# Queries and keys of two attentions, made transposed by the projection itself

## The chip, the core and the metric

One core of one Trainium2 chip runs the whole program. The metric is device time in microseconds (us) for one execution. A row of the profile names engines as PE (TensorE, matrix products), PEld (its loading of weights), DVE (VectorE), ACT (ScalarE), POOL (GpSimd) and SP (the engine that issues most DMAs).

## The reference, cut to what matters

The program is a first transformer block (gated linear attention and block attention side by side, cross attention to a memory, 32 experts) and then two hybrid layers (differential attention and stick-breaking attention side by side, a gated feed-forward), for 256 tokens of width 1024 in float32. The change touches the queries and keys of block attention (once) and of stick-breaking attention (once per layer):

```python
h = x * rsqrt(mean(x * x) + eps) * g          # per token
q_m, k_m, v_m = h @ w_in[:, 1552:2064], h @ w_in[:, 2064:2576], h @ w_in[:, 2576:3088]
o_m = moba_attention(q_m, k_m, v_m, rel_bias) # 8 heads of 64, q scaled by 64 ** -0.5
...
sq, sk, sv = h @ w_in_2[l][:, 1536:2048], h @ w_in_2[l][:, 2048:2560], h @ w_in_2[l][:, 2560:3072]
o_sb = stick_breaking_attention(sq, sk, sv)   # 8 heads of 64, scores q . k / 8
```

Both attentions need q and k with the head's 64 columns on the partitions (transposed: 4 strips of 128 columns by 256 tokens), since scores sum over them.

## The kernel before

Tokens lie in two tiles of 128 (NT = 2, T = 256). A norm (class `Norm`) keeps the transposed activations x * g, without the factor per token, in a high and a low half that together make float32 (`xs`, 8 slices of 128 by 256 tokens). The factor per token, `nrm.scale(t)`, is a column of 128 numbers, applied when a product is read out of PSUM.

A projection to 512 columns is `dense` (L324). Weights come in four chunks of 256 rows (KC = 2 slices); ScalarE makes their high half (L295, `wh`), VectorE the low half (L300, `wl`), and each pair of slices and tokens takes three matmuls (high by high, low by high, high by low, L334). Activations are stationary (128x128), 512 columns of weights move. One projection is 4 chunks x 2 token tiles x 3 x 2 slices = 48 matmuls, accumulated in two PSUM tiles of the pool `psm` (four buffers), one per token tile. In the last chunk token tile 0 is finished first and read out by `evac(0)`, then tile 1.

For queries and keys `evac` is `rows_T` (L572): the product is scaled by the token's factor into `rows` (VectorE, L267, for tile 0; ScalarE, L265, for tile 1), and TURN = 20 products later `to_T` (L566) transposes it in four 128x128 steps on TensorE (L569) and copies the result into qTm, kTm, sqT or skT (ScalarE, L570).

Work beside the projections is put among their products by hand: `soon(n, fn)` runs `fn` when n more products have been issued (`passed()` counts them), and `keep` fixes the order on an engine. TensorE runs in exactly this order. In the first block the order around the change is: projection of query (products 1 to 48), key (49 to 96), value (97 to 144), counted from the start of the query's. `gla_out(t)` (L535, output of linear attention, with a norm over its result: ScalarE L547, VectorE L549, GpSimd L178, VectorE L551) is put at 80 and 104, and `moba_scores(j)` (L598, for the head pairs j = 0 to 3) at 96 + 28 + 20 j. Both take PSUM tiles named "at" from the pool `psa`, which has two buffers: `gla_out` one, `moba_scores` two. In the layers the scores of differential attention (`diff_scores`, L1387) and later those of stick-breaking attention (L1449) are put in the same manner, and take "at" tiles too.

Two places serve as a comparison below. `decay_down` (L403) already has weights stationary and 256 tokens moving. `decay_up` has one "at" tile of two halves, and between the two products into it VectorE reads the first half:

```python
pl = new(psa, [P, NT, 256], name="at")
for t in range(NT):
    keep(mm(pl[:, t], alT[:, t * P:(t + 1) * P], wal, start=True, stop=True))           # L411
    nc.vector.scalar_tensor_tensor(la[:, t], pl[:, t], n1.scale(t), bal, ...)           # L412
```

Of the kernel before, what the change touches and what calls it, by code (L numbers as in the profile page):

```python
# [17 lines left out]
ALU = mybir.AluOpType  # L18
AX = mybir.AxisListType

P = 128
T = 256
NT = T // P
D = 1024
KD = D // P
KC = 2
# [2 lines left out]
AT_GATES = 4  # L29
AT_MERGE = (1, 1, 1, 1, 1, 1)  # L30
LAG = 3
EARLY = 24
OVER = 5
TAIL = (6, 12, 13, 15)
# [8 lines left out]
MOBA = 20  # L43
TURN = 20
# [66 lines left out]
def forward(ctx: ExitStack, tc: tile.TileContext, a: dict, out: bass.AP):  # L111
    nc = tc.nc
    mm = nc.tensor.matmul
# [9 lines left out]
    psm = ctx.enter_context(tc.tile_pool(name="psm", bufs=4, space=bass.MemoryType.PSUM))  # L123
    pst = ctx.enter_context(tc.tile_pool(name="pst", bufs=2, space=bass.MemoryType.PSUM))
    psa = ctx.enter_context(tc.tile_pool(name="psa", bufs=2, space=bass.MemoryType.PSUM))
    dram = ctx.enter_context(tc.tile_pool(name="dram", bufs=1, space=bass.MemoryType.DRAM))

    def new(pool, shape, dt=F32, name="t", **kw):
        return pool.tile(shape, dt, name=name, tag=name, **kw)
# [38 lines left out]
    cst = ctab.get  # L168
    ident = cst("ident")
# [93 lines left out]
    def scaled(dst, src, r, eng):  # L263
        if eng == "s":
            nc.scalar.activation(dst, src, AF.Copy, scale=r)  # L265
        else:
            nc.vector.tensor_scalar(dst, src, r, None, op0=ALU.mult)  # L267

    def keep(ins):
        return tc.keep_in_program_order(ins)  # L270
# [5 lines left out]
    def load(parts, kc, n, pool=wraw, tag="raw"):  # L276

        raw = chunk(pool, tag, kc, n)
        at = 0
        for src in parts:  # L280
            w = src.shape[1]
            nc.sync.dma_start(out=raw[:, :kc, at:at + w], in_=src.rearrange("(k p) n -> p k n", p=P))
            at += w
        return raw
# [18 lines left out]
    def halves(raw, kc, n, *order):  # L303

        h = high(raw, kc, n, *order)
        return h, low(raw, h, kc, n, *order)

    def wload(parts, kc, n):
        return halves(load(parts, kc, n), kc, n)
# [3 lines left out]
    def soon(n, fn, *args):  # L313

        waiting.append((products[0] + n, fn, args))

    def passed():
        products[0] += 1
        due = [v for v in waiting if v[0] <= products[0]]
        waiting[:] = [v for v in waiting if v[0] > products[0]]  # L320
        for _, fn, args in due:
            fn(*args)

    def dense(xs, parts, n, evac, tail=1, loaded=None, order=free):  # L324

        nk = len(xs)
        ps = [new(psm, [P, 512], name="mm") for _ in range(NT)]
        step = KC if n == 512 else nk
        chunks = [(k0, min(step, nk - k0)) for k0 in range(0, nk, step)]

        def go(t, k0, kc, wh, wl):
            for i, (part, ww) in enumerate(((0, wh), (1, wh), (0, wl))):
                for k in range(kc):
                    order(mm(ps[t][:, :n], xs[k0 + k][part][:, t * P:(t + 1) * P], ww[:, k, :n],  # L334
                             start=(k0 == 0 and i == 0 and k == 0), stop=(k0 + kc == nk and i == 2 and k == kc - 1)))
                    passed()

        held = []
        for c, (k0, kc) in enumerate(chunks):
            ww = wload([p[k0 * P:(k0 + kc) * P, :] for p in parts], kc, n)  # L340
            if c < len(chunks) - tail:
                for t in range(NT):
                    go(t, k0, kc, *ww)
            else:
                held.append((k0, kc, *ww))
        if loaded:
            loaded()
        for t in range(NT):
            for c in held:
                go(t, *c)  # L350
            evac(t, ps[t])

    def add_to_x(xs, W, then=None, loaded=None, order=free):
        for half in range(2):
            hs = slice(half * 512, (half + 1) * 512)

            def evac(t, ps):
                nc.vector.tensor_add(x[:, t, hs], x[:, t, hs], ps)
                if then:
                    then(x[:, t, hs], t, half)  # L360

            dense(xs, [W[:, hs]], 512, evac, 3 if half else 1, loaded and functools.partial(loaded, half), order)
# [5 lines left out]
    n1 = Norm(gmix)  # L368
# [8 lines left out]
    w_in = a["w_in"][0]  # L377
# [5 lines left out]
    me = mix1.enter_context(tc.tile_pool(name="mixe", bufs=1))  # L383
# [53 lines left out]
    def rows_into(dst, nrm):  # L437
        return lambda t, ps: scaled(dst[:, t], ps, nrm.scale(t), "sv"[t])
# [13 lines left out]
    def evac(t, pp):  # L452
        qk = new(tmp, [P, 512], name="rows")
        scaled(qk, pp, n1.scale(t), "s")
        soon(TURN, gla_turn, t, qk)
# [110 lines left out]
    def to_T(src, dst, t, scale, order):  # L566
        ps = new(pst, [P, 4, P], name="tp")
        for k in range(4):
            order(nc.tensor.transpose(ps[:, k, :], src[:, k * P:(k + 1) * P], ident))  # L569
        nc.scalar.activation(dst[:, :, t * P:(t + 1) * P], ps, AF.Copy, scale=scale)  # L570

    def rows_T(dst, nrm, scale=1.0, lag=0):  # L572
        def evac(t, pp):
            qm = new(tmp, [P, 512], name="rows")
            scaled(qm, pp, nrm.scale(t), "vs"[t])
            if lag:
                soon(lag, to_T, qm, dst, t, scale, keep)
            else:
                to_T(qm, dst, t, scale, free)
        return evac  # L580
# [11 lines left out]
    sums = new(me, [P, NT, 8], name="sums")  # L592
# [47 lines left out]
    soon(20 + 14 * 4, nmem.done)  # L640
    for t in range(NT):
        soon(TURN * 2 + 40 + 24 * t, gla_out, t)
    for i, dst in ((0, qTm), (1, kTm)):
        dense(n1.xs, [w_in[:, 1552 + 512 * i:2064 + 512 * i]], 512, rows_T(dst, n1, 0.125 if i == 0 else 1.0, TURN), order=keep)
    for j in range(4):
        soon(TURN + 8 + MOBA * j, moba_scores, j)
    dense(n1.xs, [w_in[:, 2576:3088]], 512, rows_into(vm, n1), order=keep)

    dense(nmem.xs, [w_ckv[:, 0:512]], 512, rows_T(kTc, nmem, lag=TURN), order=keep)
    dense(nmem.xs, [w_ckv[:, 512:1024]], 512, rows_into(vc, nmem), order=keep)  # L650

# [90 lines left out]
    def prefetch(n):  # L742
        ahead.extend(load_rows(src, *nextraw()) for src in itertools.islice(upcoming, n))
# [30 lines left out]
    with tc.tile_pool(name="crossp", bufs=1, reuse_waits="tile", side="right") as cp:  # L774
        qTc = new(cp, [P, 4, T], name="qTc")
        dense(n2.xs, [a["w_cq"][0]], 512, rows_T(qTc, n2, 128.0 ** -0.5), tail=2)

        pm = []
        for h in range(4):
            ps = new(psm, [P, NT, T], name="mm")  # L780
# [50 lines left out]
        def feed_moe(src, t, half):  # L831
# [14 lines left out]
            if half and t:  # L846
                logits(0, 1)

        add_to_x(slices(oT), a["w_co"][0], feed_moe, lambda half: half and prefetch(GROUP))
        ss = new(sml, [P, NT], name="s2")  # L850
        nc.vector.tensor_add(ss, ssm[:, 0], ssm[:, 1])
# [17 lines left out]
    def s3(name, n):  # L869
        return new(mp, [P, NT, n], name=name)  # L870
# [5 lines left out]
    before, ones = counting[:, 0], counting[:, 1]  # L876
# [12 lines left out]
    order, down_from = cst("order"), cst("down_from")  # L889
# [33 lines left out]
    for g in range(2):  # L923
        xsT.append(new(mp, [P, KD, GROUP * 32], name="xs%d" % g))
        if g == 0:
            wt = s3("wt", 32)
            prefetch(EARLY - GROUP)
    hT = {}
# [209 lines left out]
    sums = []  # L1138
# [188 lines left out]
    def heads8(v):  # L1327
        return v.rearrange("p (h d) -> p h d", h=8)

    def layer(l, nrm, nxt):  # L1330
        lam_init = 0.8 - 0.6 * math.exp(-0.3 * l)
        W = a["w_in_2"][l]
        tc.keep_in_program_order(nc.scalar.preload_act_table_set("natural_log_exp_and_others"))
        with tc.tile_pool(name="attp%d" % l, bufs=1, reuse_waits="tile") as ap:
# [25 lines left out]
            for i in range(2):  # L1360
                def evac(t, ps, i=i):
                    ra, rb_ = new(tmp, [P, 512], name="rows"), new(ap, [P, 512], name="th", bufs=2)
                    src, a8, b8, r = heads8(ps), heads8(ra), heads8(rb_), nrm.scale(t)

                    def times(o, v, c):
                        nc.vector.scalar_tensor_tensor(o, v, r, c.to_broadcast(list(o.shape)), op0=ALU.mult, op1=ALU.mult)

                    times(a8, src, ct[:, t:t + 1])
                    times(b8[:, :, 0:32], src[:, :, 32:64], snt[:, t:t + 1, 0:32])
                    times(b8[:, :, 32:64], src[:, :, 0:32], snt[:, t:t + 1, 32:64])  # L1370
                    nc.vector.tensor_add(ra, ra, rb_)
                    soon(TURN, to_T, ra, qkT[i], t, 0.125 if i == 0 else 1.0, keep)
# [57 lines left out]


            skT = [new(ap, [P, 4, T], name=n) for n in ("sqT", "skT")]
            for i in range(2):
                dense(nrm.xs, [W[:, 1536 + 512 * i:2048 + 512 * i]], 512, rows_T(skT[i], nrm, 0.125 if i == 0 else 1.0, TURN), order=keep)
            sv = new(ap, [P, NT, 512], name="sv")
            sqT, skT = skT
            osT = split(ap, [P, 4, T], "osT")
# [67 lines left out]
        with tc.tile_pool(name="ffnp%d" % l, bufs=1, reuse_waits="tile") as fp:  # L1505
            gT = split(fp, [P, NF, T], "gT")
            for b in range(F // 256):
                def evac(t, ps, b=b):
# [8 lines left out]
                      tail=2 if b == 0 else 1, order=keep)  # L1517
            n6 = nxt() if nxt else None
            add_to_x(slices(gT), a["w_ffn_out_2"][l], n6.feed_later if n6 else None, order=keep)
        return n6.done() if n6 else None  # L1520

    n4 = layer(0, n3, lambda: Norm(gain(a["norm_attn_2"][1])))
    class Last:

# [21 lines left out]
        def done(self):  # L1546
            return None

    layer(1, n4, Last)
    assert not waiting  # L1550

# [24 lines left out]
```

## Time and profile before

| | |
|---|---|
| median of 3 runs | 1496.31 us (1495.42 to 1499.0) |
| the profiled execution | 1499.64 us |
| its span, first to last instruction | 1498.0 us |
| TensorE busy | 1429.0 us |
| VectorE busy | 722.6 us |
| ScalarE busy | 592.0 us |

Busy times are of the profiled execution. Matmuls are pipelined: the duration of one reaches into the next, so what a stream of them costs is read from one start to another. The span has three parts: the first block's attentions up to about 280 us, the experts up to about 740 us, then the two layers of some 370 us each.

### The profile page before, as it was taken

The page shows a single profiled execution, that of the slowest core. Times are in us where ns is not written, and L with a number is a line of the kernel's source. Part 1 is how long each engine was busy: PE and PEld are TensorE (multiplying, and loading weights), DVE is VectorE, ACT ScalarE, POOL GpSimd, SP SyncE. Part 2 cuts the span into 40 slices and gives each one's busy share as a digit, 9 for nine tenths or more (in the row PEclk, how much of TensorE's full clock was granted, in tenths as well). Part 3 has the DMA queues.
Part 4 walks back from the last instruction along what each step waited for, and adds up shares of the span by engine and source line. Part 5 has one row for each costly group of instructions (what it writes and reads, how often), then busy time and mean ns, then how long its engine had stood idle before and what let it go on. Part 6 is the DMA issues. An engine that isn't in the chain of part 4 may idle for free. (4 is left out here: it accounts for less than half of the span.)

```text
span 1498.0 us, 18300 instructions
## 1 busy us (share of the span) xinstructions
PE 1429.0 (95%) x6795; PEld 937.9 (63%) x6795; DVE 722.6 (48%) x1054; ACT 592.0 (40%) x879; POOL 42.6 (3%) x59
## 2 busy tenths in 40 slices
PE   7999999999898998889899999999999999999998
PEld 5778887632121221211278788888887888888886
DVE  6675485310010000100188767666557776766654
ACT  6455554210000000000355665555454666555543
POOL 1010000000000000100000000000000000000000
PEclk9999999999999999999999999999999999999999
DMA  8744977799999999999965455666657455566663
GB/s 292 238 132 142 323 247 260 278 409 409 409 409 409 410 409 409 408 409 409 350 195 155 139 158 168 210 183 184 192 173 229 140 151 163 177 199 184 187 191 99
DMA packets 173228, 383.41 MB, mean 256 GB/s; under 512 B 13464, under 2 KB 60000, under 8 KB 172752
## 3 DMA queue, kind: packets, MB, share of 16 engines
q1 hardware_dynamic: 170480, 373.72, 71.8%
q0 software_dynamic: 1648, 6.84, 1.5%
q10 hardware_dynamic: 1008, 1.64, 0.3%
q8 instruction: 55, 0.90, 0.2%
q14 instruction: 37, 0.30, 0.1%
HBM read 381.07 MB, written 2.65 MB: 256 GB/s over the span
## 5 line engine op out<-in xcount | busy, mean ns | idle before, releaser
L300 DVE TENSOR_TENSOR wl<-raw,wh 128x1024 fp32r<-128x1024 f32 x317 | 386.8, 1223 | 218.1 <-ACT wh L295 205.1
L295 ACT ACTIVATE wh<-raw 128x1024 fp32r<-128x1024 f32 x317 | 334.5, 1059 | 283.5 <-PE mm L334 245.2
L1069 PE MATMUL mm<-raw,xs 128*32 128x512 f32 x636 | 144.7, 603 | 11.7 <-DMA raw<-in_w_exp_gate_dram 6.4
L1127 DVE TENSOR_TENSOR x<-x,tp 128x512 f32<-128x512 f32 x24 | 16.5, 687 | 266.9 <-PE tp L1126 266.9
L334 PE MATMUL mm<-wh,hAl 128*128 128x512 f32 x424 | 138.5, 408 | 0.0
L334 PE MATMUL mm<-wh,hAh 128*128 128x512 f32 x424 | 135.3, 400 | 2.6 <-ACT wh L295 2.6
L334 PE MATMUL mm<-wl,hAh 128*128 128x512 f32 x424 | 133.6, 396 | 0.0
L334 PE MATMUL mm<-wl,hBh 128*128 128x512 f32 x424 | 133.1, 394 | 0.0
L334 PE MATMUL mm<-wh,hBl 128*128 128x512 f32 x424 | 132.3, 393 | 0.2 <-DVE nlam L1352 0.2
L334 PE MATMUL mm<-wh,hBh 128*128 128x512 f32 x424 | 132.2, 393 | 0.0
L1098 PE MATMUL at<-raw,hs 128*32 128x512 f32 x276 | 85.0, 603 | 11.8 <-DMA raw<-in_w_exp_down_dram 11.8
L334 PEld LDWEIGHTS mm<-wh,hAh 128*128 128x128 f32 x424 | 79.3, 190 | 20.4 <-ACT wh L295 3.0
L334 PEld LDWEIGHTS mm<-wh,hBl 128*128 128x128 f32 x424 | 78.5, 188 | 18.2 <-issue 1.4
L334 PEld LDWEIGHTS mm<-wh,hBh 128*128 128x128 f32 x424 | 78.9, 188 | 17.5
L334 PEld LDWEIGHTS mm<-wl,hAh 128*128 128x128 f32 x424 | 79.1, 189 | 17.0
L334 PEld LDWEIGHTS mm<-wl,hBh 128*128 128x128 f32 x424 | 78.5, 188 | 16.7 <-issue 0.3
L1069 PEld LDWEIGHTS mm<-raw,xs 128*32 128x32 f32 x636 | 27.8, 109 | 96.8 <-DMA raw<-in_w_exp_gate_dram 35.6
L334 PEld LDWEIGHTS mm<-wh,hAl 128*128 128x128 f32 x424 | 75.1, 190 | 12.4 <-issue 0.8
L967 ACT COPY xs<-tp 128x512 f32<-128x512 f32 (+1 forms) x18 | 9.7, 538 | 168.2 <-PE tp L962 168.2
L1098 PEld LDWEIGHTS at<-raw,hs 128*32 128x32 f32 x276 | 14.5, 108 | 68.7 <-DMA raw<-in_w_exp_down_dram 55.8
L334 PE MATMUL mm<-wh,gTl 128*128 128x512 f32 x176 | 54.6, 391 | 0.0
L334 PE MATMUL mm<-wh,gTh 128*128 128x512 f32 x176 | 54.4, 390 | 0.0
(494 smaller groups left out, 1939.1 us busy)
## 6 DMA issues: line engine op xcount, KB each, us to landing
raw<-in_w_in_dram SPq DMA_DIRECT2D x121, 512.0 KB, 3.8
raw<-in_w_ffn_in_dram SPq DMA_DIRECT2D x176, 256.0 KB, 3.2
raw<-in_w_exp_down_dram SPq DMA_DIRECT2D x85, 512.0 KB, 10.2
raw<-in_w_exp_gate_dram SPq DMA_DIRECT2D x83, 512.0 KB, 10.2
raw<-in_w_exp_up_dram SPq DMA_DIRECT2D x76, 512.0 KB, 10.2
raw<-in_w_ffn_out_dram SPq DMA_DIRECT2D x44, 512.0 KB, 3.8
raw<-in_w_out_dram SPq DMA_DIRECT2D x24, 512.0 KB, 4.3
wh<-in_w_exp_down_dram SPq DMA_DIRECT2D x15, 512.0 KB, 10.2
```

The source lines that it names most:

```text
L295: order(nc.scalar.activation(h[:, :kc], raw[:, :kc], AF.Copy))
L300: order(eng.tensor_sub(l[:, :kc], raw[:, :kc], h[:, :kc].bitcast(F32)))
L334: order(mm(ps[t][:, :n], xs[k0 + k][part][:, t * P:(t + 1) * P], ww[:, k, :n], start=(k0 == 0 and i == 0 and k == 0), stop=(k0 + kc == nk ...
L967: keep(nc.scalar.copy(xsT[g % 2][:, k0:k0 + ps.shape[1]], ps))
L1069: keep(mm(acc[strip(j)], xsT[g % 2][:, k0 + k, strip(j)], w[:, k], start=(k0 + k == 0), stop=(k0 + k == KD - 1), skip_group_check=True))
L1098: keep(mm(Y[half][strip(j)], hT[g][:, k, strip(j)], w[:, half], start=(k == 0), stop=(k == 3), skip_group_check=True))
L1127: keep(nc.vector.tensor_add(x[:, t, hs], x[:, t, hs], ps))
```

## The change

`dense_T` makes a projection with the weights' strip of 128 columns stationary and all 256 tokens moving, so that the result is transposed as it comes: four strips j, in the halves of two PSUM tiles. `cols_T` reads a strip out on VectorE, times a constant and the tokens' factors, which now lie along the columns. `along` makes these factors as a 128x256 tile `rT`, the same on every partition: a diagonal matrix of the factors per token tile (VectorE), a product of ones with it (TensorE, ALONG = 8 products later) and a copy (ScalarE). The transposes, the `rows` and their copies fall away for these six projections. `moba_scores(j)` is put TURN = 20 products earlier, at 96 + 8 + 20 j. A product of `dense_T` is counted once per two matmuls, so 48 are counted in one projection, as before.

```diff
+    def dense_T(xs, W, evac, tail=1, order=free):
+        nk = len(xs)
+        ps = [new(psm, [P, 2, T], name="mm") for _ in range(2)]
+        chunks = [(k0, min(KC, nk - k0)) for k0 in range(0, nk, KC)]
+        def go(j, k0, kc, wh, wl):
+            for i, (part, ww) in enumerate(((0, wh), (1, wh), (0, wl))):
+                for k in range(kc):
+                    order(mm(ps[j // 2][:, j % 2], ww[:, k, j * P:(j + 1) * P], xs[k0 + k][part], start=(k0 == 0 and i == 0 and k == 0 and j % 2 == 0),
+                             stop=(k0 + kc == nk and i == 2 and k == kc - 1), skip_group_check=True))
+                    if (i * kc + k) % 2:
+                        passed()
+        held = []
+        for c, (k0, kc) in enumerate(chunks):
+            ww = wload([W[k0 * P:(k0 + kc) * P, :]], kc, 512)
+            if c < len(chunks) - tail:
+                for j in range(4):
+                    go(j, k0, kc, *ww)
+            else:
+                held.append((k0, kc, *ww))
+        for j in range(4):
+            for c in held:
+                go(j, *c)
+            evac(j, ps[j // 2][:, j % 2])
...
+    def along(nrm, pool, name="dg"):
+        dg = new(pool, [P, T], name=name)
+        for t in range(NT):
+            keep(nc.vector.tensor_scalar(dg[:, t * P:(t + 1) * P], ident, nrm.scale(t), None, op0=ALU.mult))
+        def sums():
+            ps = new(psa, [P, 512], name="at")
+            for t in range(NT):
+                keep(mm(ps[:, t * P:(t + 1) * P], cst("ones"), dg[:, t * P:(t + 1) * P], start=True, stop=True))
+            nrm.rT = new(pool, [P, T], name="rT")
+            keep(nc.scalar.copy(nrm.rT, ps[:, 0:T]))
+        soon(ALONG, sums)
+
+    def cols_T(dst, nrm, scale=1.0):
+        def evac(j, ps):
+            nc.vector.scalar_tensor_tensor(dst[:, j], ps, scale, nrm.rT, op0=ALU.mult, op1=ALU.mult)
+        return evac
...
+    soon(2, along, n1, me, "alT")
     for i, dst in ((0, qTm), (1, kTm)):
-        dense(n1.xs, [w_in[:, 1552 + 512 * i:2064 + 512 * i]], 512, rows_T(dst, n1, 0.125 if i == 0 else 1.0, TURN), order=keep)
+        dense_T(n1.xs, w_in[:, 1552 + 512 * i:2064 + 512 * i], cols_T(dst, n1, 0.125 if i == 0 else 1.0), order=keep)
     for j in range(4):
-        soon(TURN + 8 + MOBA * j, moba_scores, j)
+        soon(8 + MOBA * j, moba_scores, j)
...
+            soon(2, along, nrm, ap)
             for i in range(2):
-                dense(nrm.xs, [W[:, 1536 + 512 * i:2048 + 512 * i]], 512, rows_T(skT[i], nrm, 0.125 if i == 0 else 1.0, TURN), order=keep)
+                dense_T(nrm.xs, W[:, 1536 + 512 * i:2048 + 512 * i], cols_T(skT[i], nrm, 0.125 if i == 0 else 1.0), order=keep)
```

## Rows read from the trace of the kernel before

**Rows 1.** The page, busy time, share and instructions of each engine.

```profile
PE 1429.0 (95%) x6795; PEld 937.9 (63%) x6795; DVE 722.6 (48%) x1054; ACT 592.0 (40%) x879; POOL 42.6 (3%) x59
```

**Rows 2.** Busy time per stretch; projections of block attention, then of stick-breaking attention, first layer.

```profile
core 0: us, PE busy (x) PEld busy (x) DVE busy (x) ACT busy (x) POOL busy (x), PEclk, DMA share, GB/s
42.60:58.10 15.50, 15.50 (x83) 12.26 (x82) 11.09 (x18) 6.00 (x8) 1.14 (x2) 1.00 0.68 216
58.10:78.00 19.90, 19.90 (x97) 14.70 (x96) 12.27 (x22) 8.12 (x12) 3.61 (x3) 1.00 0.74 230
786.30:800.90 14.60, 14.60 (x78) 11.56 (x78) 14.42 (x32) 8.51 (x22) 0.00 (x0) 1.00 0.53 149
800.90:815.90 15.00, 15.00 (x84) 12.33 (x83) 11.37 (x22) 8.04 (x17) 0.00 (x0) 1.00 0.50 142
```

**Rows 3.** Timeline of TensorE: start, length, line, tiles, shapes, count; first and last of ten.

```profile
756.30 0.61 PE L334 MATMUL mm<-wh,hBh 128*128 128x512 f32 x2
...
760.38 0.61 PE L334 MATMUL mm<-wh,hAh 128*128 128x512 f32 x2
```

**Rows 4.** Timeline of TensorE: first of six groups of L403, and what follows them.

```profile
20.75 0.64 PE L403 MATMUL at<-hAh,wh 128*128 128x256 f32 x4
...
23.62 0.63 PE L334 MATMUL mm<-wh,hBl 128*128 128x512 f32 x2
```

**Rows 5.** Timeline of TensorE: one group of four transposes, and two pairs behind it.

```profile
84.41 0.60 PE L569 MATMUL tp<-c_ident,rows 128*128 128x128 f32 x4
84.77 0.71 PE L334 MATMUL mm<-wh,hAl 128*128 128x512 f32 x2
85.31 0.63 PE L334 MATMUL mm<-wl,hAh 128*128 128x512 f32 x2
```

**Rows 6.** Timeline of TensorE: four calls of float32 products, eight instructions.

```profile
33.53 1.05 PE L424 MATMUL at<-c_tri,la 128*128 128x128 f32 x8
```

**Rows 7.** Timeline around decay_up; in brackets the idle time before and who ended it.

```profile
25.56 0.69 PE L411 MATMUL at<-wal,alT 16*128 16x256 f32 x2
...
26.34 0.48 DVE L412 SCALAR_TENSOR_TENSOR la<-at,r_n,bal 128x256 f32<-128x256 f32 x1 [0.97 <-issue]
...
26.88 0.69 PE L411 MATMUL at<-wal,alT 16*128 16x256 f32 x2 [0.63 <-DVE la L412]
...
27.51 0.73 PE L334 MATMUL mm<-wl,hBh 128*128 128x512 f32 x2
```

**Rows 8.** Groups of VectorE: busy us, mean ns of one, idle before.

```profile
L300 DVE TENSOR_TENSOR wl<-raw,wh 128x1024 fp32r<-128x1024 f32 x317 | 386.8, 1223 | 218.1 <-ACT wh L295 205.1 <-PE tp L199 11.5 <-PE mm L334 0.4
```

**Rows 9.** Timeline of VectorE, end of the key projection of stick-breaking attention.

```profile
814.67 0.75 DVE L267 TENSOR_SCALAR rows<-mm,r 128x512 f32<-128x512 f32 x1 [0.44 <-PE mm L334]
```

**Rows 10.** Timeline of all engines, end of the key projection of block attention.

```profile
76.23 0.62 PE L334 MATMUL mm<-wl,hBh 128*128 128x512 f32 x2
...
78.33 0.69 DVE L551 TENSOR_TENSOR og<-at,r_g 128x512 f32<-128x512 f32 x1 [0.93 <-POOL r_g L178]
...
78.94 0.74 DVE L267 TENSOR_SCALAR rows<-mm,r_n 128x512 f32<-128x512 f32 x1
```

**Rows 11.** Timeline of all engines, from gla_out(1) to the first scores.

```profile
82.55 0.44 PE L544 MATMUL at<-st,bT 128*64 128x128 f32 x4
...
83.03 0.60 ACT L547 ACTIVATE sq<-at 128x512 f32<-128x512 f32 x1 [3.60 <-PE at L544]
...
84.63 1.01 POOL L178 TENSOR_TENSOR r_g<-v_g,mhalf 128x4 f32<-128x4 f32 x1 [6.34 <-DVE v_g L176]
...
85.92 0.68 DVE L551 TENSOR_TENSOR og<-at,r_g 128x512 f32<-128x512 f32 x1
...
88.62 0.70 PE L604 MATMUL at<-kTm,qTm 64*128 64x256 f32 x4
```

**Rows 12.** Tile bias: its last two requests; and DMA issues, KB, us to landing.

```profile
L506 POOL DMA_DIRECT2D bias<-rdram x2: 897/914/932, 61.5 to 62.4; - x2
...
bias<-rdram POOLq DMA_DIRECT2D x1, 512.0 KB, 11.0
```

**Rows 13.** Timeline of TensorE after the experts; and busy time and granted clock there.

```profile
743.91 3.78 PE L1147 MATMUL mm<-Y,selT 128*128 128x512 f32 x4 [3.46 <-ACT Y L1241]
...
742.00:750.00 8.00, 6.09 (x11) 3.45 (x12) 4.74 (x6) 6.78 (x10) 0.38 (x1) 0.57 0.91 276
```

More of the change, by code (lines that the diff above doesn't have):

```diff
@@ L31 @@
 LAG = 3
+ALONG = 8
 EARLY = 24
```

## The prediction

> **What bounds the kernel now.** I began with the busy line of the page [rows 1]: TensorE works in 1429.0 us of 1498.0. An average says little about one stage, so next I cut out the stages that the change touches, by the table of busy time per stretch [rows 2]. In each of the four stretches TensorE's busy time equals the stretch, at a granted clock of 1.00. VectorE is second: 11.09 of 15.50 us, 12.27 of 19.90, 14.42 of 14.60 and 11.37 of 15.00. So here the time is TensorE's order of work, and two things count: what an edit does to the sum of TensorE's cadences, and whether it makes TensorE wait for anybody. The second layer repeats the last two stretches, so there are six projections in all (query and key, once for block attention and twice for stick-breaking attention).
>
> The prices I read from start to start in the timeline, because a matmul's listed duration overlaps the next one's.
>
> **The matmuls.** Between 756.30 and 760.38 us stand nine pairs of 128x512 matmuls [rows 3]: 4.08 / 18 = 0.2267 us each. The old projection has 48 of them, 10.88 us. The new form (weights stationary, 256 tokens moving) already exists once in the kernel, in the decay projection: 24 matmuls from 20.75 to 23.62 us [rows 4], 0.1196 us each. The new projection has 96, 11.48 us. So +0.60 us each, +3.6 us for six. The Trainium skill, page "TensorE: Matmul & The Clock Gate", section "Back-to-back issue gap", gives columns / 2.4 + 2.5 ns; by that estimate six projections would lose only 0.7 us. The rows disagree with it: there is a fixed part of about 13 ns in this stream. I go by the rows.
>
> **The transposes.** Each old projection is followed by two groups of four. One group with the matmul pair behind it takes 85.31 - 84.41 = 0.90 us [rows 5], the pair alone 0.453 [rows 3], so a group costs 0.45. Twelve groups go: -5.4 us. Their copies on ScalarE (two per projection) and one scaling on each of ScalarE and VectorE go as well, and cost nothing now, because TensorE was never late for them in these stretches.
>
> **The scale along the columns.** Three times (block attention once, each layer once) two 128x128 float32 products are added. A float32 call shows as two instructions: the four calls of L424 are eight, in 1.05 us [rows 6]. So four instructions at 0.13 or less, plus 0.09 for the change of kind (0.54 in place of 0.453 in [rows 5]): 0.62, three times +1.9 us. The two diagonal multiplications on VectorE come eight products (some 3.6 us) earlier, the ScalarE copy of the result is wanted more than 30 products later; I cost both at nothing, with up to 1 us each time if VectorE's backlog eats that lead.
>
> So TensorE's own work comes out even: 3.6 - 5.4 + 1.9 = **+0.1 us**. What is left is waits.
>
> **Wait 1: both halves of one accumulator.** In dense_T the column strips j = 0 and 1 lie in the two halves of one PSUM tile of 2 KB per partition, 2 and 3 in another. In the last chunk the order is go(0), evac(0), go(1), evac(1), and so on: VectorE reads half 0 while go(1) wants to write half 1. The old kernel does this at one place, decay_up: two calls of L411 write the halves of tile pl, and VectorE's L412 reads the first half between them. There TensorE stopped [rows 7]: first pair at 25.56, VectorE from 26.34 for 0.48, second pair only at 26.88, marked idle behind L412, though nothing that L412 writes is an input of it. So a read of one half holds up a write to the other. The Trainium skill, page "PSUM — Partial Sum Buffer", section "PSUM bank collisions raise a hardware error", says that semaphores should guard PSUM by bank and quadrant and not by address, because two engines in one bank collide even in different columns. The trace agrees with it (the stop at 26.88), and it speaks against this change.
>
> The price: 26.88 - 25.56 = 1.32 us from pair to pair, against 0.24 in flow (two times 0.12), so 1.08 with an idle VectorE; the next matmul follows only 0.63 later, up to 0.3 more. The new matmuls end sooner after their start than float32 ones, which takes some 0.15 off. I take 1.05, bounds 0.8 and 1.4. Two such waits stand in each projection (before go(1) and go(3)), twelve in all: 12.6 us. TensorE takes its work in order, so everything behind go(1) waits too: the rest of the chunk, the attention steps put among the products, the next projection.
>
> To this comes VectorE's own queue. evac(0) waits behind whatever runs there, mostly the 1.22 us subtraction for the weights' low halves [rows 8], and VectorE is busy 72, 62, 99 and 76% [rows 2]. With a half-done instruction of some 0.45 us in three of four cases that is 0.35 a wait, 4.2 us. Old read-outs show both ends: at 814.67 an idle VectorE began at once when TensorE was done [rows 9]; in the block attention's key projection the last product of token tile 0 started at about 76.46 (second of the pair at 76.23), and VectorE read it at 78.94, behind a product that waited for GpSimd [rows 10], some 2.1 us late. In the old kernel nobody waited for that; now TensorE would. I add 1.0 for it, half its size, as the order on VectorE may come out either way. Sum of wait 1: 12.6 + 4.2 + 1.0 = **+17.8 us**, bounds 9.6 (twelve at 0.8) and 24 (twelve at 2.0).
>
> VectorE's added work (24 read-outs of 0.48 or less for 6 scalings of 0.74, six diagonals) is some +1.2 us per projection. Where it is busy 14.42 of 14.60 us this wouldn't fit, but that stretch grows by the waits, about 3 us, so I add nothing.
>
> **Wait 2: the scores come 20 products earlier.** moba_scores(0) moves from product 28 to product 8 of the value projection. gla_out(1) was put at product 104 counted from the query projection, and that is product 8 too, ahead of the scores. Each head pair of moba_scores takes two "at" tiles, gla_out takes one, and there are two. In the old trace [rows 11] gla_out(1) ended on TensorE at about 82.9; its tile is read by ScalarE at 83.03, its norm goes through GpSimd at 84.63, and VectorE's last read starts at 85.92 and takes 0.68, to 86.60. The scores started at 88.62, after it. Moved, they issue at about 82.9: the first head finds a tile (0.3 us), the second waits until 86.6: **+3.4 us**, bounds 0 (a free tile after all) and 4.5. Behind it on TensorE stands the whole value projection. Their other parts per pair (two additions and two maxima on VectorE, four exponentials on ScalarE) pass the same queues 9 us earlier; they issue no DMA. The bias that they add was requested at 62.4 and took 11.0 us [rows 12], so 73.4, in time. Starting earlier buys nothing: TensorE was full anyway.
>
> Sum: 0.1 + 17.8 + 3.4 = +21.3 us on the profiled execution's 1499.64 us. That execution is 0.2% above the median of 1496.31; the added microseconds are the same, so I forecast 1496.3 + 21 = **1517 us**. No stage hides this: in the first block the expert weights are requested in an order tied to TensorE's, so a delay there moves the experts too, and both layers are bound by TensorE.
>
> **Rivals.**
> 1. *No wait at the halves.* The two halves are disjoint columns, and if only overlapping columns are ordered, go(1) runs while evac(0) reads. Place: before go(1) and go(3). It decides as soon as all twelve are gone: then 0.1 + 3.4 = +3.5, 1500 us, within what can't be told from no change. Against it stands [rows 7], one instance but the same layout; for it, that in dense_T only the first half's product carries the start flag.
> 2. *VectorE's queue is worse.* With evac(0) behind two instructions each time, a wait costs 2.2 us: 26 us, with wait 2 and 2 us for late scales 1528 us. For it: 99% in [rows 2], and [rows 10].
> 3. *The clock falls in wait 2.* After a stop of 3.46 us at 743.91 the granted clock averaged 0.57 over 742 to 750 [rows 13], the lower of the two levels, 1.2 GHz, for most of it: 8 x 0.43 = 3.4 us lost. The stop of wait 2 is as long: 1520 us. The Trainium skill, page "TensorE: Matmul & The Clock Gate", says that an idle array falls to half rate, and the row agrees.
>
> **How the numbers follow.** Forecast, its own range 1508 to 1523: 0.56. Rival 3: 0.12, rival 2: 0.15, rival 1: 0.12. For something that gains and that I don't see: 0.05, nearly all of it as "faster". The range 1504 to 1531 leaves out rival 1, the gain, and some of rival 2's end. This kernel's measurement tells 0.3%, 4.5 us, from no change: faster 0.04, same 0.11 (most of rival 1), slower 0.85.
>
> **What would show it.** Right: TensorE idle before go(1) and go(3), released by the new read-out on VectorE, twelve times, 0.9 to 1.6 us from last start to next start; one stop of 3 to 4 us at the first scores, released by the last read of gla_out's tile; 128x256 matmuls 0.12 us apart; the six stretches without transposes. Wrong: TensorE without gaps in the tails, or read-outs that start after go(1). Above all the twelve waits carry the sum; if they are half as long, the time is 1508.

## The result and the profile after

The changed kernel takes 1516.5 us (median of 4 runs, 1514.54 to 1519.85) against 1497.65 us for the kernel before in the same measurement: ratio 1.0127, interval 1.0114 to 1.0140. Forecast were 1517 us. A second measurement of the pair (e10 below) gave 1519.33 and 1498.33 us, ratio 1.0142 (1.0121 to 1.0162). The profiled execution of the changed kernel took 1514.54 us, its span is 1512.8 us, 14.8 us more than the span before. The two profiled executions lie closer together than the medians do: the one before is 2 us above its median, this one 2 us below.

The page's busy line, which answers to [rows 1]:

```profile
PE 1430.5 (95%) x7047; PEld 951.0 (63%) x7047; DVE 727.0 (48%) x1072; ACT 584.4 (39%) x870; POOL 41.6 (3%) x59
```

TensorE is as busy as before, 1430.5 us for 1429.0, in 252 more instructions. So nearly all of the added time is idle time and not work. The view of waits, for TensorE (engine and line <- who ended it: us in total, times, longest), has five lines that the kernel before doesn't have; L363 is the matmul of `dense_T`, L617 the read-out in `cols_T`, L652 the score product of `moba_scores`, L579 the last step of `gla_out`:

```profile
PE mm L363 <- DVE sqT L617: 4.2, 4, 1.6
...
PE at L652 <- DVE og L579: 2.8, 1, 2.8
...
PE mm L363 <- DVE kTm L617: 2.6, 2, 2.1
PE mm L363 <- DVE qTm L617: 2.5, 2, 1.9
PE mm L363 <- DVE skT L617: 2.1, 4, 0.5
```

Twelve stops behind read-outs, 11.4 us of idle time, and one stop of 2.8 us at the scores. The end of the key projection of block attention shows both lengths of a stop (timeline; in brackets the idle time before and who ended it):

```profile
79.28 0.40 PE L363 MATMUL mm<-hBh,wl 128*128 128x256 f32 x2
...
80.72 0.69 DVE L579 TENSOR_TENSOR og<-at,r_g 128x512 f32<-128x512 f32 x1 [1.15 <-POOL r_g L179]
81.33 0.41 DVE L617 SCALAR_TENSOR_TENSOR kTm<-mm,rT 128x256 f32<-128x256 f32 x1
...
81.80 0.50 PE L363 MATMUL mm<-hBh,wh 128*128 128x256 f32 x2 [2.12 <-DVE kTm L617]
...
83.09 0.40 PE L363 MATMUL mm<-hBh,wl 128*128 128x256 f32 x2
...
83.53 0.42 DVE L617 SCALAR_TENSOR_TENSOR kTm<-mm,rT 128x256 f32<-128x256 f32 x1 [0.29 <-PE mm L363]
84.01 0.50 PE L363 MATMUL mm<-hBh,wh 128*128 128x256 f32 x2 [0.52 <-DVE kTm L617]
84.35 0.40 PE L363 MATMUL mm<-hBl,wh 128*128 128x256 f32 x2
```

The short stop is the pure one: VectorE waits for TensorE, reads at once, and TensorE goes on 0.06 us after the read. TensorE's last matmul started at 83.21 (second of the pair at 83.09), the next at 84.01: 0.80 us in place of 0.12, and the pair behind it takes 0.34 in place of 0.24. So 0.78 us, of which the profile calls 0.52 idle. The long stop is the same with VectorE's queue in front: the read-out stands behind `og`, which waits for GpSimd, as in [rows 10]; there nobody waited for it. Of the twelve, eight are short, and four long (2.12, 1.94, 1.60 and 1.59 us idle). In front of the other three long ones stands the subtraction for the weights' low halves, for one of them:

```profile
808.68 1.21 DVE L301 TENSOR_TENSOR wl<-raw,wh 128x1024 fp32r<-128x1024 f32 x1
809.81 0.41 DVE L617 SCALAR_TENSOR_TENSOR sqT<-mm,rT 128x256 f32<-128x256 f32 x1
```

At the scores (timeline, then busy time and granted clock of a stretch, columns as in [rows 2]):

```profile
89.72 0.70 PE L652 MATMUL at<-kTm,qTm 64*128 64x256 f32 x2
...
91.44 1.01 POOL L179 TENSOR_TENSOR r_g<-v_g,mhalf 128x4 f32<-128x4 f32 x1 [10.75 <-DVE v_g L177]
...
92.48 0.69 DVE L579 TENSOR_TENSOR og<-at,r_g 128x512 f32<-128x512 f32 x1 [1.12 <-POOL r_g L179]
93.22 0.48 PE L652 MATMUL at<-kTm,qTm 64*128 64x256 f32 x1 [2.81 <-DVE og L579]
...
94.07 1.09 PE L335 MATMUL mm<-wh,hAl 128*128 128x512 f32 x2
...
94.00:98.00 4.00, 4.00 (x12) 3.15 (x11) 3.23 (x5) 2.81 (x9) 1.31 (x3) 0.57 0.34 46
```

This is the chain of [rows 11], with the scores now in front of its end: the first head's product runs, the second waits until VectorE has read gla_out's tile. Behind the stop a pair of 128x512 matmuls takes 0.88 us from start to start in place of 0.453, at a granted clock of 0.57: for most of four microseconds TensorE had the lower of its two levels, 1.2 GHz. By the granted clock that costs some 4 x 0.43 = 1.7 us.

TensorE's own prices (timeline):

```profile
45.08 0.61 PE L609 MATMUL at<-alT,c_ones 128*128 128x128 f32 x4
45.45 0.49 PE L363 MATMUL mm<-hAl,wh 128*128 128x256 f32 x2
45.77 0.40 PE L363 MATMUL mm<-hAh,wl 128*128 128x256 f32 x2
...
50.69 0.40 PE L363 MATMUL mm<-hBh,wh 128*128 128x256 f32 x2
...
53.80 0.40 PE L363 MATMUL mm<-hBl,wh 128*128 128x256 f32 x2
```

Thirteen pairs start one behind the other from 50.69 to 53.80: 0.1196 us a matmul, the price of [rows 4]. The sums of ones with the pair behind them take 0.69, less 0.24 for the pair: 0.45 us, not 0.62.

The stages, from the starts in the traces (us; "pairs" and "pairs, old place" are the experiments e1 and e3 below):

| from ... to | before | changed | pairs | pairs, old place |
|---|---|---|---|---|
| bias product (L496 before) to first matmul of the memory's keys | 46.97 | 58.72 | 52.57 | 45.95 |
| first differential to first stick-breaking scores, layer 0 | 42.19 | 45.88 | 41.67 | 41.69 |
| the same, layer 1 | 42.21 | 45.87 | 41.67 | 41.67 |

In the first line some 1.8 us in "changed" and "pairs" is moved work: the scores that stand in this stretch now are missing behind it, where these two kernels win back 1.8 us up to the first transpose of linear attention's output (`tp<-c_ident,og`; 53.26 for 55.05 us). With that, the three stretches are 9.96 + 3.69 + 3.66 = 17.3 us longer in the changed kernel's trace.

### The profile page after: what moved, and what is told of

The parts are those of the page before. It is cut to its first block, busy times and chain, and to the rows that moved or that the text cites. A ratio compares the mean times of both kernels' runs of the same rounds, so it can differ in the third digit from the quotient of the medians.

```text
span 1512.8 us, 18810 instructions
## 1 busy us (share of the span) xinstructions
PE 1430.5 (95%) x7047; PEld 951.0 (63%) x7047; DVE 727.0 (48%) x1072; ACT 584.4 (39%) x870; POOL 41.6 (3%) x59
## 5 line engine op out<-in xcount | busy, mean ns | idle before, releaser
L335 PE MATMUL mm<-wh,hAl 128*128 128x512 f32 x376 | 123.1, 408 | 0.0
L335 PE MATMUL mm<-wh,hAh 128*128 128x512 f32 x376 | 120.5, 401 | 2.6 <-ACT wh L296 2.6
L335 PE MATMUL mm<-wl,hAh 128*128 128x512 f32 x376 | 118.0, 395 | 0.0
L335 PE MATMUL mm<-wh,hBl 128*128 128x512 f32 x376 | 117.3, 393 | 0.3 <-DVE nlam L1401 0.3
L335 PE MATMUL mm<-wh,hBh 128*128 128x512 f32 x376 | 117.3, 393 | 0.3 <-ACT hBh L204 0.3
L335 PE MATMUL mm<-wl,hBh 128*128 128x512 f32 x376 | 117.2, 391 | 0.0
L335 PEld LDWEIGHTS mm<-wh,hAh 128*128 128x128 f32 x376 | 70.5, 191 | 18.1 <-ACT wh L296 3.0
L335 PEld LDWEIGHTS mm<-wh,hBh 128*128 128x128 f32 x376 | 69.9, 188 | 16.2 <-ACT hBh L204 0.7
L335 PEld LDWEIGHTS mm<-wl,hBh 128*128 128x128 f32 x376 | 70.3, 188 | 15.3 <-issue 0.3
L335 PEld LDWEIGHTS mm<-wh,hBl 128*128 128x128 f32 x376 | 69.6, 188 | 16.3 <-issue 1.4
```

## The experiments

The theory: (a) twelve stops, because two halves of one PSUM tile are written and read in turn; (b) one stop at the scores, because gla_out still holds one of two "at" tiles; (c) TensorE's own work comes out even. The rivals were a slower matmul stream, a delay that the experts swallow, and VectorE as the bound.

**e1: read-outs in pairs.**

```diff
         for j in range(4):
             for c in held:
                 go(j, *c)
-            evac(j, ps[j // 2][:, j % 2])
+            if j % 2:
+                for i in (j - 1, j):
+                    evac(i, ps[i // 2][:, i % 2])
```

> The changed kernel, but the two halves of one PSUM tile are read out only after both are written (go(0), go(1), then evac(0), evac(1); the same for 2 and 3). TensorE's own order stays the same. Theory of the halves: the twelve stops go. In the changed kernel's trace TensorE stands 11.4 us idle behind the twelve read-outs, and each stop hides some 0.26 us more (the 0.28 us of the last matmul, less its 0.12 in flow, and a 0.10 us slower restart), 14.5 us in all: 1516.5 - 14.5 = 1502 us, no idle of TensorE before L363. Rival, the time went to a slower stream of matmuls and not to stops: no change, 1513 to 1518 us.

Measured: 1501.3 us (11 runs), ratio to before 1.002 (1.0011 to 1.0029). That is 15.2 us less than the changed kernel's median. In the waits of TensorE none is left before `dense_T`'s matmuls; of the five lines above one remains:

```profile
PE at L654 <- DVE og L581: 2.8, 1, 2.8
```

The layers' stretches fall from 45.88 to 41.67 us. TensorE's order is the same in both kernels, so the stops are the cost, not the form of the matmuls.

**e2: the scores at their old place**, with the stops at the halves still there.

```diff
-        soon(8 + MOBA * j, moba_scores, j)
+        soon(TURN + 8 + MOBA * j, moba_scores, j)
```

> The changed kernel with moba_scores(j) at its old place (20 products later); dense_T and its read-outs as changed. Theory of the buffer: the stop of 2.81 us before the first scores goes (some 3.3 us with the slow restart), and so does the stretch of half clock behind it (0.56 and 0.58 over 94 to 98 us, 1.7 us lost): 1516.5 - 5 = 1511.5 us, granted clock 1.00 there, the twelve stops at the halves still there. Rival, a delay in the first block is taken up again by the experts' transfers: the stop goes from the trace, the time stays 1515 to 1517 us.

Measured: 1518.51 us, not 1511.5. The stop at the scores was gone from the trace, and nothing was gained. In this profile the clock had fallen earlier, behind the first stop in the query projection, where order, stops and their lengths (1.95 and 0.52 us) are those of the changed kernel, and once more behind the stops of the key projection. Two stretches after the first and one after the second, in this run:

```profile
62.00:66.00 4.00, 3.48 (x17) 3.19 (x16) 1.18 (x3) 0.23 (x1) 1.83 (x2) 0.50 0.55 144
66.00:70.00 4.00, 4.00 (x14) 2.94 (x14) 1.74 (x3) 0.82 (x1) 0.00 (x0) 0.50 1.01 347
...
90.00:94.00 4.00, 3.48 (x13) 2.91 (x13) 1.43 (x4) 1.06 (x1) 0.00 (x0) 0.50 0.36 131
```

and in the changed kernel's:

```profile
62.00:66.00 4.00, 4.00 (x30) 3.48 (x29) 3.13 (x7) 1.66 (x2) 1.82 (x2) 1.00 0.54 146
```

The same order of work with and without a fall of the clock. The size can be read from e11, which is the same program: in its trace the clock stays at 1.00, and the table's first stretch takes 52.09 us, in this one 60.69. So the two falls cost this execution (1522.13 us) 8.6 us there, more than the 5 that the edit should bring. The median of e2 alone decides nothing; e7, e10 and e11 took it up.

**e3: both edits.**

> Both edits together: read-outs in pairs, and the scores at the old place. What is left of the change is its work on TensorE: 256-column matmuls, no transposes, the sums of ones. Theory: this sum is +0.1 us, so the time is that of the kernel before, within 3 us. Rival, the transposes were hidden and cost nothing: +3.6 for the matmuls and +1.9 for the sums are not paid back, 5.5 us more than before. Rival, VectorE's additional read-outs hold the weights' low halves back in the fullest stretch: 2 to 5 us more than before, with TensorE waiting for wl there.

Measured: 1496.69 us (11 runs) against 1498.10 (23 runs), ratio 0.9991 (0.9982 to 1.0000). So what is left of the change, its own work on TensorE, is worth -1.4 us, at the edge of what can be told from nothing; no rival holds. In the traces each layer's stretch is 0.5 us shorter than before, and the first block's 1.0 us. Against e1 the scores' new place costs 1501.3 - 1496.7 = 4.6 us.

**e4: the scores in the middle**, `soon(18 + MOBA * j, moba_scores, j)`.

> The changed kernel with moba_scores(j) 10 products later than in the change (and 10 earlier than before): 4.5 us, while the stop was 2.81 us. Theory of the buffer: by then gla_out's tile has been read, so the stop and the half clock go as in the run with the old place: 1511.5 us. Rival, any place earlier than the old one costs, because the scores' work on VectorE and ScalarE meets that of the norm and the value projection: between 1512 and 1516 us, with TensorE waiting for another engine there.

Measured: 1515.38 us, in six runs from 1510.69 to 1522.21. The stop has shrunk from 2.81 to 0.7 us, not vanished, and the clock fell in the query projection again. The two shortest runs, 1510.69 and 1511.15, have a mean granted clock of 0.997 and 0.996, the two longest 0.989. With the clock moving this much the median tells nothing, though it lies in the rival's range; the two shortest agree with the theory, but for the 0.7 us that are left of the stop.

**e5: the tiles in turn**, strip j in tile j % 2, each still read right behind its product.

```diff
-  mm(ps[j // 2][:, j % 2], ..., start=(... and j % 2 == 0), ...)
+  mm(ps[j % 2][:, j // 2], ..., start=(... and j < 2), ...)
...
-            evac(j, ps[j // 2][:, j % 2])
+            evac(j, ps[j % 2][:, j // 2])
```

> The changed kernel, but strip j goes to PSUM tile j % 2 (half j // 2), each read out right behind its product as in the change. TensorE's order is the same; between a read-out and the next write into its tile lie six matmuls of the other tile, 0.72 us. Theory of the shared tile: with VectorE idle the read-out is over 0.80 us after the last start, so a stop shrinks from 0.80 to about 0.1 us; behind a busy VectorE the longer ones (up to 2.1 us) keep 0.5 to 1.4 us. Before go(1) and go(3) no stops, before go(2) some 3 us in six projections: 1516.5 - 12 = 1504 us. Rival, any read-out by VectorE in the last chunk holds TensorE up, whichever tile it reads: 1513 to 1518 us.

Measured: 1507.48 us, ratio 1.0068 (1.0054 to 1.0082). 9 us of the 15 come back, less than the 12 expected. What is left is one stop in each projection, before go(2) or, unlike expected, before go(3), long where VectorE's queue stands in front:

```profile
PE mm L363 <- DVE sqT L617: 2.5, 2, 1.2
...
PE mm L363 <- DVE kTm L617: 1.4, 1, 1.4
...
PE mm L363 <- DVE skT L617: 0.5, 2, 0.2
PE mm L363 <- DVE qTm L617: 0.4, 1, 0.4
```

The read-out still happens at the same place, and TensorE runs through the next strip: so it isn't a read-out as such that stops it, but one in the tile that it writes next. Six matmuls between cover most of a short stop (0.2 us are left before `skT`) and not a long one (1.2 and 1.4 us before `sqT` and `kTm`).

**e6 and e7: TensorE kept busy in the stops**, five matmuls into a tile that nobody reads; e7 has the scores at the old place as well.

```diff
             evac(j, ps[j // 2][:, j % 2])
+            if j % 2 == 0:
+                pd = new(psm, [P, 512], name="mm")
+                for _ in range(5):
+                    order(mm(pd[:, 0:T], xs[0][0][:, 0:P], xs[0][0], start=True, stop=True))
```

> The changed kernel with five extra 256-column matmuls (0.60 us), into a PSUM tile that nobody reads, between go(0) and go(1) and between go(2) and go(3). They add work and shorten no wait; TensorE is busy for most of each stop. If the stop itself is the cost (the read-out's 0.8 us, whatever TensorE does meanwhile): 1515 to 1518 us, as the changed kernel. If part of the cost is the clock that falls behind the stops of the first block (in the trace with the scores at their old place it fell there for 13.7 us): 1512 to 1514 us and granted clock 1.00 in both projections of the first block; the clock may still fall behind the stop at the scores.

> The same five extra matmuls per stop, and the scores at their old place. Theory, that the old place brought nothing in the earlier run because the clock fell at the halves' stops in that run: with TensorE busy there it shows its gain, some 5 us below the filled run with the scores at the new place, 1508 to 1511 us. Rival, the old place brings nothing as long as the halves' stops are there: equal to the filled run within 1.5 us.

Measured: 1515.92 us (1514.03 to 1516.66) and 1510.94 us (1510.22 to 1512.22). The first is the changed kernel's time: a stop costs what the read-out takes, whatever TensorE does meanwhile. (In the four long stops TensorE is still idle for 1.0 to 1.5 us behind the five matmuls.) But its four runs lie within 2.6 us, where the changed kernel's nine lie within 9.1 and its first four within 5.3, and in its trace the clock is 1.00 in both projections of the first block; it falls behind the scores alone. All eight runs of e6 and e7 have a mean granted clock of 0.993 or more; of the changed kernel's nine, four are below. The second is 5.0 us below the first, and their runs don't overlap, as theory (b) says: with TensorE busy for most of the stops at the halves, the old place of the scores shows its gain.

**e8: the same at the scores**, on top of e1: 22 such matmuls ahead of the score product that waits.

> Read-outs in pairs, the scores at the new place, and 22 extra 256-column matmuls (2.6 us), into a tile that nobody reads, ahead of the score product that waits for gla_out's tile. The stop stays, but TensorE is busy in it. With read-outs in pairs, the new place cost 1501.3 - 1496.7 = 4.6 us: some 3 for the stop and, by theory, 1.7 for the half clock behind it. So 1499.6 us and a granted clock of 1.00 at the scores. Rival, the clock is no part of it: 1501 to 1502 us.

Measured: 1500.14 us (11 runs) against e1's 1501.3: 1.2 us less, where 1.7 were expected. The medians can't carry this. The runs of either differ by more (1498.54 to 1502.57, and 1499.31 to 1503.21), and the kernel before, measured beside each, was 0.8 us faster beside e8 (1497.27) than beside e1 (1498.10): both ratios are 1.002 (1.0011 to 1.0029). What can be told is in the traces. In e1:

```profile
88.00:92.00 4.00, 4.00 (x12) 3.09 (x11) 3.26 (x5) 2.60 (x8) 1.51 (x3) 0.57 0.34 46
```

and in e8, with the fill and the stretch after it:

```profile
84.08 2.90 PE L658 MATMUL mm<-hAh 128*128 128x256 f32 x22
...
88.00:92.00 4.00, 4.00 (x18) 3.29 (x18) 3.05 (x6) 3.42 (x10) 1.05 (x2) 1.00 0.26 43
```

The clock stays at 1.00, and 18 instructions fit where 12 did. The table's first stretch takes 50.97 us in e8 and 52.57 in e1, 1.6 less. So in these traces, one execution each, the 4.6 us at the scores are about 3 for the stop and 1.6 for the clock behind it.

**e9: the factors without TensorE**, on top of e3: `along` writes the two columns of factors to DRAM and reads them back on all partitions, by DMAs of GpSimd's queue.

```diff
+        for t in range(NT):
+            nc.gpsimd.dma_start(out=rd[t * P:(t + 1) * P].rearrange("(p o) -> p o", o=1), in_=nrm.scale(t))
+        nc.gpsimd.dma_start(out=nrm.rT, in_=bass.AP(tensor=rd.tensor, offset=rd.offset, ap=[[0, P], [1, T]]))
```

> Read-outs in pairs and the scores at the old place, and the tile rT made without TensorE: the factors go to DRAM and come back on all partitions by three DMAs on GpSimd's queue, in place of diagonals, products of ones and copies. Those products cost TensorE 0.45 us each time (45.08 to 45.77 us in the changed kernel's trace, less one pair in flow), three times: 1496.7 - 1.4 = 1495.3 us, below both kernels. Rival, the transfers come late or hold up GpSimd's other work (the norm of gla_out, the bias of the block attention): TensorE waits before the first read-outs, 1498 us or more.

Measured: 1507.67 us, 11 us more than e3. The rival holds, at another place than I named: `rT` was never late, but the weights were.

```profile
28.70 1.06 ACT L296 ACTIVATE wh<-raw 128x1024 fp32r<-128x1024 f32 x1 [6.47 <-DMA raw<-in_w_in_dram]
...
31.46 1.22 PE L441 MATMUL at<-wal,alT 16*128 16x256 f32 x2 [4.78 <-DVE la L442]
...
35.63 0.55 POOL L608 DMA_DIRECT2D rT<-rdalT  x1 [13.60 <-DMA rdalT<-r_n]
```

Behind two requests of 128 factors each GpSimd waited 13.60 us, and in this time ScalarE waited 6.47 us for a chunk of weights; VectorE's read-out in decay_up came late behind it, and TensorE stood. That accounts for some 5.6 of the 11 us (the bias product starts at 55.44 us, in e3 at 49.87); most of the rest is lost before the first layer's scores, and its cause stays open. In the layers' stretches the saving is there: 41.24 and 41.23 us for e3's 41.69 and 41.67. No version beat both kernels by more than e3's 1.4 us.

**e10 and e11: the changed kernel and e2 once more**, side by side.

> The changed kernel once more, beside the next run, for the spread of its times and of its mean granted clock. Theory: single runs between 1513 and 1520 us, the longer ones with the lower mean clock, median 1515 to 1518 us.

> The changed kernel with the scores at the old place, once more. Theory: runs in which the clock does not fall behind the halves' stops of the first block come to 1511 to 1512 us, the others to 1515 us and more, with a lower mean clock; so single runs spread over 1511 to 1522 us, and at an equal mean clock they lie 4 to 6 us below the changed kernel's. Rival, the old place brings nothing while the halves' stops are there: no run below 1514 us, and no difference at an equal clock.

Measured: 1519.33 and 1514.17 us. All runs of both kernels by their mean granted clock:

| clock | changed (9 runs) | scores at the old place (9 runs) |
|---|---|---|
| 0.995 and more | 1514.37, 1514.54, 1514.59, 1515.35 | 1510.16, 1510.94 |
| 0.990 to 0.993 | 1517.65, 1519.33, 1519.43, 1519.85 | 1514.17, 1514.90, 1515.51, 1516.83, 1516.90 |
| under 0.990 | 1523.48 | 1520.12, 1522.13 |

At an equal clock the old place is some 3 to 4 us ahead in the two upper rows, and the fastest runs are just below those of the theory (1511 to 1512). The rival, no gain while the halves' stops are there, is out. The traces of two runs in which the clock didn't fall at the halves agree: from the bias product to the first transpose of `og` the changed kernel takes 111.98 us and e11 107.13, 4.85 less. e2's first median had drawn four runs with a fallen clock.

## Why the prediction was right

The time, the side and the mechanism were right: 21 us were forecast, 18.9 and 21.0 measured. The terms were less exact than the sum, and part of the agreement is luck: the stops were sized too high, and falls of the clock that the sum doesn't hold made up for it in about half of the runs.

- **TensorE's own work, +0.1 forecast: -1.4 us (e3).** The price of the new matmuls was right to the nanosecond. The sums of ones were sized by a bound (0.62) and cost 0.45, which explains 0.5 us of the difference; the rest isn't resolved. The diagonals and the copy of `rT`, put at nothing, held: no wait of TensorE or of the read-outs names them.
- **Wait 1, +17.8 forecast: 14.5 us by the trace, 15.2 by e1's median (13.3 from the changed kernel's runs without falls of the clock at the halves).** Twelve stops at the two places named, before go(1) and go(3). VectorE's queue was forecast at 5.2 us (4.2 and 1.0), and the four long stops exceed the short ones by 5.2 (1.60 + 1.42 + 1.08 + 1.07); that the sizes agree is luck, since the forecast spread the queue over nine of twelve stops. The bare stop was mis-sized: 1.05 us taken, 0.78 measured, just under the lower bound of 0.8. The step that failed is the reading of [rows 7]. The prediction took 1.32 us from pair to pair as the stop, less 0.24 for two matmuls in flow. But that pair's own two instructions start 0.32 us apart (25.56 and 25.88 in the trace) and not 0.12, so 0.20 of it is no stop. From the last matmul's start to the next start it is 1.01 us there and 0.80 here: the matmul lasts 0.37 and here 0.28, VectorE begins 0.09 and here 0.04 after its end and reads for 0.48 and here 0.42. The restart, taken as up to 0.3, costs 0.10.
- **Wait 2, +3.4 forecast: 4.6 us.** The stop was some 3, as worked out from [rows 11]. The rest is rival 3, which came true beside the forecast, at half its price: 4 us of low clock and not 8. (The 8 us of [rows 13] also hold the end of the idle stop itself, 742 to 743.91.)
- **What the sum lacks:** the clock also falls behind the halves' stops, in some runs and not in others, which moves the changed kernel between 1514.4 and 1523.5 us. Runs without it are 17 us above before, which is -1.4 + 14.5 + 4.6 = 17.7. I had put the clock only at the scores.
- **Rivals.** Rival 1 (no wait at the halves) is out by the waits. Rival 2 (two instructions ahead of each read-out, 2.2 us a wait) is out by the eight short stops. That VectorE's fuller queue wouldn't bind in its fullest stretch held, but not for the reason given (that the stretch grows by the waits): with the stops gone that stretch got shorter than before, and TensorE waited for nothing in it.
- Not tried: whether go(1) could run beside the read of the other half if nothing ordered them. The wait is one of the program's semaphores, so no run here shows what the chip would do without it.

## What to carry to other kernels

Where one engine sets the time, look for the read that sits between two writes of one PSUM tile: it costs that engine a full round trip (here 0.78 us with an idle reader, up to 2.4 with a queue in front), and reading both halves after both are written cost nothing here (e3). Work that is put earlier in a hand-made order meets whoever holds its buffers at the new place; ask that for each pool before moving it. And a stop has a second price in the clock behind it, which varied here from run to run, so that a median of a few runs can hide a gain of 4 us.

## What the runs showed of the hardware

The granted clock fell behind a stop of 1.9 us in the query projection in two traces (e2, e4) and not in three others (the changed kernel, e10, e11), with the same order of work up to there; between e2 and e11, the same program, that was 8.6 us. With five small matmuls inside each stop the time stayed as it was and the spread was 2.6 us in four runs, for 9.1 in nine; 22 ahead of the scores kept the clock at 1.00 in e8's trace. Two requests that move 128 single numbers each (e9) held their queue for 13.6 us, and in that time ScalarE waited 6.47 us for weights; that the one caused the other was not tested apart.
